# A gated three-branch decoder layer on one core: its output projection in two units of seven products

## The chip, the core and the metric

The kernel runs on one core of a Trainium2 chip. The metric is the device time of one execution in microseconds (us); less is better.

## What is computed

One layer on 512 rows of width 2048, in float32. RMSNorm of the input, one wide input projection (w_in), three mixers of width 1024 whose results are projected to 2048 (w_br_a, w_br_b, w_br_c), a gated sum of the three, the output projection w_o with the residual, and a last RMSNorm. Cut to what matters here:

```python
h = rmsnorm(x, norm_g)
proj = h @ w_in                       # split into ten parts
y_a, y_b, y_c = ...                   # three mixers, each ending in @ w_br_*
g = sigmoid(gates.reshape(bsz, seq, 3, D_MODEL))
merged = g[:, :, 0] * y_a + g[:, :, 1] * y_b + g[:, :, 2] * y_c
x = x + merged @ w_o
return rmsnorm(x, final_g)
```

## The kernel before

Each float32 operand is split into a high and a low part in the type float32r (ScalarE casts the high part, VectorE subtracts to get the low one), and a product is made as three: high by high, low by high, high by low. A matmul has 128 rows of the left operand (the stationary side) and 512 columns of weights; P is 128, CH is 512, a weight block (`rawA`, `rawB`) is 128 by 1024 and holds two steps of 128 channels.

**The input projection** is done in 15 units of 1024 columns. A unit multiplies a 2 by 2 block matrix by a 2 by 2 block matrix in seven products instead of eight (Strassen's way in Winograd's form); `PRODUCTS` (line 58) lists them: 11, s1, s2, s4, s3, 12, 22, with the buffer of each (A or B) and how its weights come: "load" is a plain transfer on SyncE's queue (line 130), "add" a transfer on GpSimd's queue that adds a block to the one in the buffer (line 132), "sum" an addition on VectorE (line 140). `unit` (line 423) runs a product of 8 channel steps by 2 row tiles by 3 matmuls = 48 matmuls, collects results in pairs of PSUM banks (X, Z, V), copies some out (`snap`, ScalarE, line 442), adds others to them (`join`, VectorE, line 447) and hands each finished quarter to a callback (on11, on12, on21, on22). The operands of the left side (the rows of h and their sums and differences) are made once, by `make` and `operand` (lines 349 to 390), and live in `sets`, 28 buffers of the pool `xp`.

**The weights** go through the class `Weights`. `plan` sets when a block is transferred: four blocks ahead of its split, an "add" after the split of what stood in the buffer. `split_to` (line 147) splits a block into `wh` (ScalarE, line 160) and `wl` (VectorE, line 161), two blocks ahead of TensorE and at a raised priority, into three pairs of buffers (`parts`); `place` says into which pool.

**The branches.** `branch` (line 877) multiplies a mixer's result by its projection, 4 groups of 512 columns, 4 row tiles in 4 banks, 96 matmuls a group, and folds in the gates on VectorE (lines 900, 901) into `merged`. The last branch calls `merge_done`, which turns the merged rows into columns on TensorE (`turned`, line 538, 16 transposes a group) and splits them into the high and low operands `m`.

**The output projection** takes the four groups of 512 columns of w_o one after the other: 16 channel steps by 4 row tiles by 3 matmuls, lines 960 to 962. For the last group all weights are split ahead into free buffers, and the row tiles are done one by one (lines 986 to 988), the last one in two halves of 256 columns that have a bank each. `finish` (line 930) adds the residual (line 936), squares and sums on ScalarE (line 937), multiplies by final_g (line 938) and adds up (line 940); after the last group of a row tile comes its root (ScalarE), reciprocal and a Newton step (VectorE), the scaling of its four pieces, two on each engine, and their stores.

**The order on each engine** is set by Tile's scheduler when the program is built, by priority (the order of the code; splits are raised by 300 places) and by its own estimate of when an instruction can start. On the chip each engine then runs its list in that order, and a waiting instruction holds all behind it. `feed` puts queued work (`soon`, `add`) between the steps of the products, at a rate.

## Time and profile before

| | us |
|---|---|
| median of three executions | 1673.27 |
| lowest, highest | 1665.56, 1676.21 |
| the profiled execution, its time | 1667.63 |
| its span (first to last instruction on the core) | 1665.8 |

The rows further down are of the profiled execution, times in us from the start of its span. PE is TensorE (PEld its weight loads), DVE VectorE, ACT ScalarE, POOL GpSimd, SP SyncE; L160 is line 160. Lengths of matmuls overlap, so their pace is read from starts. A name in brackets after an instruction is what ended the idle time of its engine before it.

### The profile page before, as it was taken

The page shows a single profiled execution, that of the slowest core. Times are in us where ns is not written, and L with a number is a line of the kernel's source. Part 1 is how long each engine was busy: PE and PEld are TensorE (multiplying, and loading weights), DVE is VectorE, ACT ScalarE, POOL GpSimd, SP SyncE. Part 2 cuts the span into 40 slices and gives each one's busy share as a digit, 9 for nine tenths or more (in the row PEclk, how much of TensorE's full clock was granted, in tenths as well). Part 3 has the DMA queues.
Part 4 walks back from the last instruction along what each step waited for, and adds up shares of the span by engine and source line. Part 5 has one row for each costly group of instructions (what it writes and reads, how often), then busy time and mean ns, then how long its engine had stood idle before and what let it go on. Part 6 is the DMA issues. An engine that isn't in the chain of part 4 may idle for free.

```text
span 1665.8 us, 19674 instructions
## 1 busy us (share of the span) xinstructions
PE 1633.9 (98%) x7332; PEld 1347.9 (81%) x7332; DVE 1131.3 (68%) x1387; ACT 740.9 (44%) x931; POOL 160.4 (10%) x191
## 2 busy tenths in 40 slices
PE   7899999999999999999999999999999999999997
PEld 5688887888888888888888888888888888888886
DVE  4866699899889969967878885656733544543342
ACT  6756443444444555556645554445622221222322
POOL 1201011110202020101010101111000000000000
PEclk9999999999999999999999999999999999999999
DMA  9978685868777797789989998699984644443302
GB/s 305 237 195 192 176 189 118 227 149 204 153 200 146 200 209 186 175 239 244 296 201 260 227 285 181 176 224 252 240 292 152 197 144 139 127 139 94 105 17 101
DMA packets 111440, 316.04 MB, mean 190 GB/s; under 512 B 12273, under 2 KB 16497, under 8 KB 111345
## 3 DMA queue, kind: packets, MB, share of 16 engines
q1 hardware_dynamic: 63392, 179.50, 33.7%
q0 software_dynamic: 26496, 96.48, 31.3%
q10 hardware_dynamic: 21456, 38.82, 6.4%
q8 instruction: 57, 0.93, 0.2%
q14 instruction: 39, 0.31, 0.1%
HBM read 279.09 MB, written 35.65 MB: 189 GB/s over the span
## 4 chain that ended last, share of the span: by engine, by line
PE 87%; issue 6%; DMA 3%; DVE 2%; POOL 1%; ACT 1%; SPq 0%; ACTq 0%; POOLq 0%; DVEq 0%
PE X L436 12%; PE X L434 12%; PE X L435 11%; PE y L888 5%; PE y L887 5%; PE y L886 5%; PE Z L436 5%; PE Z L434 5%; PE Z L435 5%; PE V L435 3%; PE V L434 3%; PE V L436 3%; PE o L961 3%; PE o L960 3%; PE o L962 3%
## 5 line engine op out<-in xcount | busy, mean ns | idle before, releaser
L161 DVE TENSOR_TENSOR wl<-rawA,wh 128x1024 fp32r<-128x1024 f32 (+1 forms) x281 | 341.6, 1217 | 220.0 <-ACT wh L160 218.2
L160 ACT CAST wh<-rawA 128x1024 fp32r<-128x1024 f32 (+1 forms) x281 | 294.8, 1050 | 408.7 <-PE X L435 113.4
L161 DVE TENSOR_TENSOR wl<-rawB,wh 128x1024 fp32r<-128x1024 f32 x220 | 268.3, 1221 | 237.9 <-ACT wh L160 231.9
L160 ACT CAST wh<-rawB 128x1024 fp32r<-128x1024 f32 x220 | 231.0, 1052 | 358.9 <-PE y L887 102.4
L434 PE MATMUL X<-wh,x 128*128 128x512 f32 x480 | 188.1, 393 | 6.9 <-ACT x L351 6.7
L132 POOL DMA_DIRECT2D rawA<-wts x124 | 107.3, 865 | 896.4 <-DVE wl L161 860.6
L434 PE MATMUL X<-wh,xs 128*128 128x512 f32 x480 | 187.8, 391 | 4.7 <-ACT wh L160 4.6
L435 PE MATMUL X<-wh,x 128*128 128x512 f32 x480 | 187.7, 391 | 1.2 <-DVE x L352 1.2
L435 PE MATMUL Z<-wh,xs 128*128 128x512 f32 x480 | 187.1, 390 | 0.7 <-DVE xs L352 0.7
L434 PE MATMUL Z<-wh,xs 128*128 128x512 f32 x480 | 186.6, 390 | 1.1 <-ACT xs L351 1.1
L435 PE MATMUL X<-wh,xs 128*128 128x512 f32 x480 | 187.3, 390 | 0.0
L436 PE MATMUL X<-wl,xs 128*128 128x512 f32 x480 | 168.8, 391 | 5.8 <-DVE wl L161 5.8
L436 PE MATMUL X<-wl,x 128*128 128x512 f32 x480 | 172.6, 394 | 0.0
L436 PE MATMUL Z<-wl,xs 128*128 128x512 f32 x480 | 169.9, 391 | 0.0
L572 DVE SCALAR_TENSOR_TENSOR conv<-v,prm,conv 128x511 f32<-128x511 f32 (+14 forms) x240 | 168.5, 727 | 0.0
L886 PE MATMUL y<-wh,u 128*128 128x512 f32 x384 | 149.9, 390 | 0.0
L887 PE MATMUL y<-wh,u 128*128 128x512 f32 x384 | 149.7, 390 | 0.0
L888 PE MATMUL y<-wl,u 128*128 128x512 f32 x384 | 149.6, 390 | 0.0
L434 PEld LDWEIGHTS X<-wh,x 128*128 128x128 f32 x480 | 90.2, 189 | 27.3 <-ACT x L351 7.8
L436 PEld LDWEIGHTS X<-wl,xs 128*128 128x128 f32 x480 | 89.6, 188 | 26.7 <-DVE wl L161 8.3
L434 PEld LDWEIGHTS X<-wh,xs 128*128 128x128 f32 x480 | 90.3, 188 | 25.1 <-ACT wh L160 6.3
L435 PEld LDWEIGHTS X<-wh,x 128*128 128x128 f32 x480 | 90.5, 189 | 20.9 <-DVE x L352 2.3
(172 smaller groups left out, 2349.5 us busy)
## 6 DMA issues: line engine op xcount, KB each, us to landing
rawB<-wts SPq DMA_DIRECT2D x160, 512.0 KB, 4.4
rawA<-wts POOLq DMA_DIRECT2D x124, 512.0 KB, 6.7
rawA<-wts SPq DMA_DIRECT2D x99, 512.0 KB, 4.2
rawB<-wts POOLq DMA_DIRECT2D x60, 512.0 KB, 8.8
g<-g SPq DMA_DIRECT2D x48, 256.0 KB, 4.5
d<-turn ACTq DMA_DIRECT2D x32, 256.0 KB, 5.8
g<-snap ACTq DMA_DIRECT2D x24, 256.0 KB, 5.2
g<-gate ACTq DMA_DIRECT2D x24, 256.0 KB, 5.6
```

Of the source, the lines that this page charges most:

```text
L132: self.nc.gpsimd.dma_start(out=self.raw[key], in_=self.src[b], accum_op=ALU.add)
L160: self.nc.scalar.copy(out=h[:, at], in_=raw[:, at])
L161: self.nc.vector.tensor_tensor(out=l[:, at], in0=raw[:, at], in1=h[:, at].bitcast(F32), op=ALU.subtract)
L434: T.matmul(p, lhsT=xh, rhs=h, start=start and k == 0, stop=False, skip_group_check=True)
L435: T.matmul(p, lhsT=xl, rhs=h, start=False, stop=False, skip_group_check=True)
L436: T.matmul(p, lhsT=xh, rhs=l, start=False, stop=k == KB - 1, skip_group_check=True)
L572: V.scalar_tensor_tensor(out=c[:, s:], in0=v[:, : S - s], scalar=pcol(P_BW, i * CONV_B + CONV_B - 1 - s), in1=c[:, s:], op0=ALU.mult, op1= ...
L886: T.matmul(banks[t], lhsT=uh[:, tk], rhs=h, start=k == 0, stop=False)
L887: T.matmul(banks[t], lhsT=ul[:, tk], rhs=h, start=False, stop=False)
L888: T.matmul(banks[t], lhsT=uh[:, tk], rhs=l, start=False, stop=k == KB - 1)
L960: T.matmul(pt[t], lhsT=mh[:, tk], rhs=h, start=k == 0, stop=False)
L961: T.matmul(pt[t], lhsT=ml[:, tk], rhs=h, start=False, stop=False)
```

## The change

The output projection becomes two more units of `PRODUCTS`, each of 1024 columns of w_o, over the merged rows as the left operand, which has 2 by 2 blocks as well: 256 rows by 1024 channels. The rows of w_o are packed in another order (`WO_ROWS`), so that a block's channels come from the column groups 0 and 2, or 1 and 3, and operands can be made as soon as two groups of the last branch are merged. `quarter` turns merged rows into raw quarters (`got`, 256 columns a half, in the pool of small tiles), and `derive` makes an operand from them, as `make` did for the input. In the last branch those of the first two channel pairs are made, in the first output unit those of the others. `finish` takes a sign and adds a product by it. The second unit hands its last product to `last`: its weights are split into buffers of `xp`, tile 2 is finished in one piece, tile 3 in two halves of the same bank.

```diff
 def stages():
     out = []
+    def seven(u, products):
+        for name, tag, what, row, col in products:
+            key = (u, tag, name == "12")
+            out.extend((tag, key + (s,), what, block(u, row, col, s)) for s in range(STEPS))
...
+    for u in range(2):
+        seven(WO_UNIT + u, PRODUCTS)
     return out
...
-    def unit(on11, on12, on21, on22, each=lambda n: None, first=False):
+    def unit(on11, on12, on21, on22, each=lambda n: None, first=False, end=None):
...
+        if end:
+            end(X)
+            return
         run("22", X, False)
...
+    def quarter(cg, i):
+        j, rows = 2 * (cg // 2) + i, cg % 2
+        got = [tmp("m").rearrange("p (c t) -> p c t", c=2) for _ in range(2)]
+        for c in range(2):
+            p = turned([merged[t][cg] for t in range(NT)], 2 * i + c)
+            for h in range(2):
+                A.copy(out=got[h][:, c], in_=p[:, half[h]])
+        quarters[j][rows], quarters[j][rows + 2] = got
     def merge_done(cg):
...
+        if cg == 3:
+            return
+        for i in range(2):
+            soon(0.1, quarter, cg, i)
+        if cg == 1:
+            for j in range(2):
+                for p in FIRST:
+                    add(0.7 if p[0] in ("11", "12", "22") else 1.4, lambda name=p[0], j=j: derive(name, j, *quarters[j]))
...
-    def finish(t, cg, p, lo=0, hi=CH):
+    def finish(t, cg, p, sign, lo=0, hi=CH):
...
-        V.tensor_tensor(out=y[:, at], in0=p, in1=y[:, at], op=ALU.add)
+        V.scalar_tensor_tensor(out=y[:, at], in0=p, scalar=sign, in1=y[:, at], op0=ALU.mult, op1=ALU.add)
...
+    def residual(t, u):
...
+        for cg in (2 * u, 2 * u + 1):
+            nc.sync.dma_start(out=ys[t, cg], in_=xn[t, :, cg * CH : (cg + 1) * CH])
+    def out_each(u):
+        work = {}
+        if u == 0:
+            work[1], work[2] = (lambda: quarter(3, 0)), (lambda: quarter(3, 1))
...
+                work[3 + n] = lambda name=name, j=j: derive(name, j, *quarters[j])
+            work[18] = final_g
...
+    def last(X):
+        ws = [w.next() for _ in range(KB)]
+        for i, p in enumerate(X):
+            step = CH if i == 0 else CH // 2
+            for lo in range(0, CH, step):
+                at = slice(lo, lo + step)
+                for k, (h, l) in enumerate(ws):
...
+                    T.matmul(p[:, at], lhsT=xh, rhs=h[:, at], start=False, stop=False, skip_group_check=True)
...
+                finish(i + 2, 2, p[:, at], 1.0, lo, lo + step)
+            store(i + 2)
+    def place(n, base=len(w.stages) - STEPS):
+        return (xp, "x", "x") if n >= base else (parts, "wh", "wl")
+    w.place = place
+    for u in range(2):
+        def on_left(t, src, u=u):
+            finish(t, 2 * u, src, 1.0)
+            if u and t < 2:
+                store(t)
+        unit(
+            on_left, lambda t, src, u=u: finish(t, 2 * u + 1, src, -1.0), on_left,
+            lambda t, src, u=u: finish(t, 2 * u + 1, src, -1.0), each=out_each(u), end=last if u else None,
+        )
```

Three places in the order of the built programs. First, ScalarE where weights are split ahead of need into buffers of `xp`: before, in the third column group of the output projection (wh494 to wh498 are of the last group).

```order
L160 CAST wh486_11990<-rawA486_11832 128x1024 [waits DMAHW3_49,PE_49,Activation_49]
L937 ACTIVATE sq_862_11972,s_863_11973<-y_856_11854 128x512 [waits DVE_49]
L937 ACTIVATE sq_864_11978,s_865_11979<-y_857_11856 128x512 [waits DVE_49]
L160 CAST wh494_12262<-rawA494_12108 128x1024 [waits DMAHW3_49]
L160 CAST wh487_12020<-rawB487_11870 128x1024 [waits DMAHW0_49,PE_49,Activation_49]
L160 CAST wh495_12268<-rawB495_12146 128x1024 [waits DMAHW0_49]
L160 CAST wh496_12272<-rawA496_12176 128x1024 [waits DMAHW4_49]
L160 CAST wh488_12050<-rawA488_11900 128x1024 [waits DMAHW5_49,PE_49,Activation_49]
L160 CAST wh497_12276<-rawB497_12206 128x1024 [waits DMAHW2_49]
```

The same after, in the second output unit, from the end of s1 to the start of s4's fourth step (wh504 to wh507 are s2's weights, wh508 to wh511 s4's, wh520 to wh523 those of the last product, whose buffers rawA496 to rawA499 get an accumulating transfer first; DMASW is GpSimd's queue).

```order
L170 CAST wh506_12266<-rawA498_12030 128x1024 [waits DVE_49,PE_49]
L450 COPY snap_911_12262<-Z_909_12193 128x512 [waits PE_49]
L170 CAST wh520_12552<-rawA496_11980 128x1024 [waits DMASW0_49]
L170 CAST wh507_12282<-rawA499_12048 128x1024 [waits DVE_49,PE_49]
L170 CAST wh521_12568<-rawA497_11998 128x1024 [waits DMASW1_49]
L170 CAST wh508_12304<-rawB508_12114 128x1024 [waits DVE_49,PE_49]
L170 CAST wh522_12628<-rawA498_12030 128x1024 [waits DMASW2_49]
L170 CAST wh509_12327<-rawB509_12133 128x1024 [waits DVE_49,PE_49]
L170 CAST wh523_12632<-rawA499_12048 128x1024 [waits DMASW3_49,PE_49]
L450 COPY snap_916_12343<-X_904_12111 128x512 [waits PE_49]
L170 CAST wh510_12348<-rawB510_12152 128x1024 [waits DMAHW5_49,DVE_49,PE_49]
L450 COPY snap_917_12344<-X_905_12112 128x512 [waits PE_49]
```

The splits made ahead waited for plain loads (DMAHW); now they wait for accumulating transfers, between casts of s2 and s4.

Second, TensorE at the seam of the two halves of the last row tile: before (o_901 and o_904 are two banks),

```order
L986 MATMUL o_901_12506<-wh499_12284,m_837_11459 128x256
L987 MATMUL o_901_12506<-wh499_12284,m_837_11459 128x256
L988 MATMUL o_901_12506<-wl499_12285,m_837_11459 128x256
L986 MATMUL o_904_12561<-wh492_12178,m_781_10901 128x256 [waits DVE_49]
L987 MATMUL o_904_12561<-wh492_12178,m_781_10901 128x256
L988 MATMUL o_904_12561<-wl492_12179,m_781_10901 128x256
```

and after (X_905 is one bank).

```order
L1027 MATMUL X_905_12112<-wh523_12632,x22_869_11653 128x256
L1028 MATMUL X_905_12112<-wh523_12632,x22_869_11653 128x256
L1029 MATMUL X_905_12112<-wl523_12633,x22_869_11653 128x256
L1027 MATMUL X_905_12112<-wh520_12552,x22_815_11203 128x256 [waits DVE_49]
L1028 MATMUL X_905_12112<-wh520_12552,x22_815_11203 128x256
L1029 MATMUL X_905_12112<-wl520_12553,x22_815_11203 128x256
```

The second half went into a bank of its own; now it follows the first one in the same bank, and waits for VectorE.

Third, VectorE near the end: before, the last row tile, whose halves are read at the first and fourth row,

```order
L936 TENSOR_TENSOR y_885_12294<-o_901_12506,y_885_12294 128x256 [waits PE_49]
L938 TENSOR_TENSOR y_885_12294<-y_885_12294,fgb_825_11391 128x256 [waits Activation_49]
L940 SCALAR_TENSOR_TENSOR ssum3_11706<-s_903_12556,ssum3_11706 128x1
L936 TENSOR_TENSOR y_885_12294<-o_904_12561,y_885_12294 128x256 [waits PE_49]
L938 TENSOR_TENSOR y_885_12294<-y_885_12294,fgb_825_11391 128x256 [waits Activation_49]
L940 SCALAR_TENSOR_TENSOR ssum3_11706<-s_906_12611,ssum3_11706 128x1
L992 RECIPROCAL s_907_12616<-s_908_12617 128x1 [waits Activation_49]
L993 SCALAR_TENSOR_TENSOR s_908_12617<-s_907_12616,ssum3_11706 128x1 [waits DVE_49]
L994 TENSOR_SCALAR s_908_12617<-s_908_12617 128x1 [waits DVE_49]
L995 TENSOR_TENSOR s_907_12616<-s_907_12616,s_908_12617 128x1 [waits DVE_49]
L1001 TENSOR_SCALAR y_841_11576<-y_841_11576,s_907_12616 128x512 [waits DVE_49]
L1001 TENSOR_SCALAR y_873_12132<-y_873_12132,s_907_12616 128x512
```

and after, from the sums of product 12 in the second unit (y_912 is row tile 0, y_913 tile 1, y_915 tile 3; X_905 is the bank of tile 3).

```order
L455 TENSOR_TENSOR snap_906_12188<-V_926_12516,snap_906_12188 128x512 [waits PE_49]
L455 TENSOR_TENSOR snap_907_12189<-V_927_12517,snap_907_12189 128x512 [waits PE_49]
L970 SCALAR_TENSOR_TENSOR y_912_12292<-snap_906_12188,y_912_12292 128x512 [waits DVE_49]
L970 SCALAR_TENSOR_TENSOR y_913_12301<-snap_907_12189,y_913_12301 128x512 [waits DMAHW7_49,DVE_49]
L972 TENSOR_TENSOR y_912_12292<-y_912_12292,fgb_874_11696 128x512 [waits Activation_49]
L974 SCALAR_TENSOR_TENSOR ssum0_11848<-s_929_12586,ssum0_11848 128x1
L970 SCALAR_TENSOR_TENSOR y_915_12323<-X_905_12112,y_915_12323 128x256 [waits DMAHW3_49,PE_49]
L982 RECIPROCAL s_930_12591<-s_931_12592 128x1 [waits Activation_49]
L983 SCALAR_TENSOR_TENSOR s_931_12592<-s_930_12591,ssum0_11848 128x1 [waits DVE_49]
L984 TENSOR_SCALAR s_931_12592<-s_931_12592 128x1 [waits DVE_49]
L972 TENSOR_TENSOR y_913_12301<-y_913_12301,fgb_874_11696 128x512 [waits Activation_49]
L974 SCALAR_TENSOR_TENSOR ssum1_11856<-s_933_12608,ssum1_11856 128x1
```

Before, the closing steps of a row tile stood together; now those of tiles 0 and 1 stand around the read of tile 3's first half.

## Rows read from the trace of the kernel before

**Rows 1.** The page: the span, and engines' busy time, share, instructions.
```profile
span 1665.8 us, 19674 instructions
...
PE 1633.9 (98%) x7332; PEld 1347.9 (81%) x7332; DVE 1131.3 (68%) x1387; ACT 740.9 (44%) x931; POOL 160.4 (10%) x191
```

**Rows 2.** Stretches: start:end, length, busy by engine (instructions), TensorE's granted clock, DMA share, GB/s.
```profile
1000.00:1200.00 200.00, 200.00 (x884) 165.62 (x883) 122.36 (x116) 106.07 (x126) 27.68 (x32) 1.00 0.86 215
1337.00:1480.30 143.30, 143.30 (x657) 118.83 (x656) 69.06 (x88) 32.49 (x37) 0.00 (x0) 1.00 0.48 147
1480.30:1656.90 176.60, 176.60 (x833) 148.17 (x832) 67.59 (x106) 49.32 (x76) 0.00 (x0) 1.00 0.25 78
```

**Rows 3.** Groups by line, 1480.3 to 1666: count, busy us, mean ns, idle before.
```profile
L960 PE MATMUL o<-wh,m 128*128 128x512 f32 x192 | 74.9, 390 | 0.0
...
L986 PE MATMUL o<-wh,m 128*128 128x512 f32 x48 | 18.7, 389 | 0.0
...
L986 PE MATMUL o<-wh,m 128*128 128x256 f32 x32 | 9.1, 283 | 0.0
```

**Rows 4.** TensorE in order of time: start, length, line, tiles.
```profile
1480.34 0.39 PE L960 MATMUL o<-wh,m 128*128 128x512 f32 x1
...
1645.38 0.28 PE L986 MATMUL o<-wh,m 128*128 128x256 f32 x1
...
1656.77 0.28 PE L988 MATMUL o<-wl,m 128*128 128x256 f32 x1
```

**Rows 5.** VectorE in order of time, from 1480.
```profile
1480.38 0.69 DVE L900 TENSOR_TENSOR g<-y,g 128x512 f32<-128x512 f32 x1
1480.99 0.68 DVE L901 TENSOR_TENSOR m<-m,g 128x512 f32<-128x512 f32 x1
...
1482.79 1.22 DVE L161 TENSOR_TENSOR wl<-rawA,wh 128x1024 fp32r<-128x1024 f32 x1
1483.92 0.68 DVE L901 TENSOR_TENSOR m<-m,g 128x512 f32<-128x512 f32 x1
```

**Rows 6.** Line 132, all accumulating transfers of GpSimd's queue: issue to landing, us.
```profile
DMA to landing us min/median/max: 5.3/7.6/12.8
```

**Rows 7.** Last gate unit, in order of time: TensorE's s2 begins, GpSimd's transfers.
```profile
1159.02 0.86 POOL L132 DMA_DIRECT2D rawA<-wts  x1 [14.87 <-DVE wl L161]
...
1159.30 0.39 PE L434 MATMUL X<-wh,xs 128*128 128x512 f32 x1
...
1164.60 0.86 POOL L132 DMA_DIRECT2D rawA<-wts  x1 [1.83 <-DVE wl L161]
```

**Rows 8.** ScalarE in the same stretch.
```profile
1161.99 1.05 ACT L160 CAST wh<-rawA 128x1024 fp32r<-128x1024 f32 x1 [0.63 <-PE X L435]
...
1170.70 1.05 ACT L160 CAST wh<-rawB 128x1024 fp32r<-128x1024 f32 x1
```

**Rows 9.** Landing of the transfers issued at 1159.02 and at 1164.60.
```profile
DMA to landing us min/median/max: 5.6/5.6/5.6
...
DMA to landing us min/median/max: 8.1/8.1/8.1
```

**Rows 10.** VectorE after TensorE's last full products and after its last.
```profile
1645.58 0.69 DVE L936 TENSOR_TENSOR y<-o,y 128x512 f32<-128x512 f32 x1 [6.65 <-PE o L988]
1647.06 0.69 DVE L938 TENSOR_TENSOR y<-y,fgb 128x512 f32<-128x512 f32 x1 [0.79 <-ACT sq L937]
...
1657.09 0.42 DVE L936 TENSOR_TENSOR y<-o,y 128x256 f32<-128x256 f32 x1 [4.26 <-PE o L988]
...
1659.49 0.16 DVE L995 TENSOR_TENSOR s<-s,s 128x1 f32<-128x1 f32 x1
```

**Rows 11.** ScalarE, 1480.3 to 1666: the load of a function table.
```profile
L991 ACT ACT_TABLE_LOAD x1 | 1.3, 1283 | 0.0
```

**Rows 12.** ScalarE at the end, in order of time.
```profile
1659.68 1.33 ACT L999 ACTIVATE y<-y,s 128x512 f32<-128x512 f32 x2 [0.87 <-DVE s L995]
1660.44 0.95 ACTq L1002 DMA_DIRECT2D out<-y  x2
```

More of the change, by code (lines that the diff above doesn't have):

```diff
@@ L364, in less, with derive @@
             V.scalar_tensor_tensor(out=out, in0=in0, scalar=sign, in1=in1, op0=ALU.mult, op1=ALU.subtract)
+    def derive(name, j, x11, x12, x21, x22):
+        if name == "s1":
+            qs[j] = tmp("q").rearrange("p (c t) -> p c t", c=2)
+            less(qs[j], x22, x21)
+        elif name == "s2":
+            less(qs[j], x11, qs[j], -1.0)
+        elif name == "s4":
+            less(qs[j], qs[j], x12, -1.0)
+        elif name == "s3":
+            less(x11, x11, x21)
+        operand(name, j, {"11": x11, "12": x12, "22": x22, "s3": x11}.get(name, qs[j]))
     def make(name, j):
@@ L874, in trunk @@
     merged = [[None] * 4 for _ in range(NT)]
-    m = [None] * KD
     def branch(b, u, done=None):
@@ L943, in finish, with store @@
             V.tensor_scalar(out=ssum[t], in0=s, scalar1=1.0 / D, scalar2=RMS_EPS, op0=ALU.mult, op1=ALU.add)
[L945 to L989 removed]
+    def store(t):
         a, r, n = ssum[t], small(), small()
@@ L1002, in trunk @@
             (nc.scalar if c % 2 else nc.sync).dma_start(out=out[t, :, c * CH : (c + 1) * CH], in_=y)
+    def residual(t, u):
+        if u == 0:
+            ys[t, 0], ys[t, 1] = tmp("y"), tmp("y")
+        else:
+            pair = slot(F32, "y")
+            ys[t, 2], ys[t, 3] = pair[:, 0], pair[:, 1]
+        for cg in (2 * u, 2 * u + 1):
+            nc.sync.dma_start(out=ys[t, cg], in_=xn[t, :, cg * CH : (cg + 1) * CH])
+    def out_each(u):
+        work = {}
+        if u == 0:
+            work[1], work[2] = (lambda: quarter(3, 0)), (lambda: quarter(3, 1))
+            rest = [(p[0], j) for p in FIRST[1:] for j in (2, 3)]
+            rest.sort(key=lambda r: [p[0] for p in PRODUCTS].index(r[0]) if r[0] not in ("12", "22") else 9)
+            for n, (name, j) in enumerate(rest):
+                work[3 + n] = lambda name=name, j=j: derive(name, j, *quarters[j])
+            work[18] = final_g
+        for t in range(NT):
+            work[19 + t] = lambda t=t: residual(t, u)
+        return lambda n: work.get(n, lambda: None)()
@@ new lines, in last @@
+    def last(X):
[5 more added lines that the diff above has]
+                for k, (h, l) in enumerate(ws):
+                    x = sets["22"][k // 2][:, k % 2]
+                    xh, xl = (x[:, o + i * P : o + (i + 1) * P] for o in (0, HT))
+                    end = k == KB - 1
+                    T.matmul(p[:, at], lhsT=xh, rhs=h[:, at], start=False, stop=False, skip_group_check=True)
+                    T.matmul(p[:, at], lhsT=xl, rhs=h[:, at], start=False, stop=False, skip_group_check=True)
+                    T.matmul(p[:, at], lhsT=xh, rhs=l[:, at], start=False, stop=end, skip_group_check=True)
+                finish(i + 2, 2, p[:, at], 1.0, lo, lo + step)
+            store(i + 2)
@@ L1012, in pack, with seven @@
     import numpy as np
-    col = chunked(w_in)
     out = []
-    for _, left, right in UNITS:
-        for row in range(2):
-            for at in (left, right):
-                out.append(col[row * STEPS : (row + 1) * STEPS, at // CH])
+    def seven(col, columns):
+        for left, right in columns:
+            for row in range(2):
+                for at in (left, right):
+                    out.append(col[row * STEPS : (row + 1) * STEPS, at // CH])
+    seven(chunked(w_in), [u[1:] for u in UNITS])
+    for a in (w_a, w_c, w_b):
+        out.append(chunked(a).transpose(1, 0, 2, 3).reshape(-1, P, RAW))
+    rows = w_o.reshape(KD, P, D)[[k for half in WO_ROWS for k in half]].reshape(D, D)
+    seven(chunked(rows), [(RAW * u, RAW * u + CH) for u in range(2)])
     gw = group_w.reshape(len(WINDOWS), 2, P, CG).transpose(0, 2, 1, 3).reshape(2, 2, P, CH)
     out.append(gw.transpose(0, 2, 1, 3).reshape(2, P, RAW))
-    for a in (w_a, w_c, w_b, w_o):
-        out.append(chunked(a).transpose(1, 0, 2, 3).reshape(-1, P, RAW))
     return np.concatenate(out)
```

94 lines of the change are left out of this document (20 added, 74 removed).

## The prediction

> **What bounds the kernel now.** I read the page's busy times first, then the stretches, then groups by line, then single engines in order of time. TensorE is busy 1633.9 of 1665.8 us [rows 1], and the stretches show it without a gap: 200.00 of 200.00 us in a stretch of input units, 143.30 of 143.30 in the last branches, 176.60 of 176.60 in the output projection, each at a granted clock of 1.00, which is the 2.4 GHz level [rows 2]. So whatever stage I look at, its matmuls set the time, and work taken from TensorE is worth its full price as long as nothing new makes it wait. VectorE has much room in the output projection (67.59 us of 176.6) and less in the units (122.36 of 200) [rows 2]. The change makes output units of the first kind out of the second, so I look for waits that the new order can make.
>
> **What goes.** The old projection runs 3 x 192 + 3 x 48 = 720 products of 512 columns and 3 x 32 = 96 of 256 [rows 3]. The busy lengths (390 and 283 ns) overlap; the pace is read from starts. From 1645.38 to 1656.77 the 96 short ones take 11.39/95 = 0.120 us each [rows 4]. From 1480.34 to 1645.38 there are 165.04 us for 720 long ones and 16 transposes [rows 4]; twelve long ones in a row stand 2.72 us after one another, 0.2266 each, 163.15 in all, which leaves 0.118 for a transpose. The new projection has 2 x 7 x 8 x 6 = 672 products, 24 of them cut in two halves: 648 long and 48 short. The transposes stay 64 in all, 16 of them after the branch. Removed: 72 x 0.2266 + 48 x 0.120 = 16.3 + 5.8 = **22.1 us** of TensorE, all of it on the path. The program is the same, engine by engine, until the second column group of the last branch, so nothing before some 1413 us moves.
>
> **What I cost at nothing.** Sixteen operands and eight differences are made in the last branch. VectorE is busy there 69.06 of 143.30 us and ScalarE 32.49 [rows 2]; 24 more operations of 0.605 on VectorE, 14.5 us, fit into the last two column groups (43 us) beside their 16 merges and 8 splits (19 us). If they did not, the weights' low halves would come late by the overhang. The transfers: the output stage goes from 32 plain loads of 512 KB to 24 plain and 24 adding, where the engines of the DMA are busy a quarter of the time (share 0.25 [rows 2]). The residual's rows move from ScalarE's queue to SyncE's, ahead of weights of later products there; the first unit's wait for its last operands, some 34 us after the branch, and what stands behind them is needed 20 us later still.
>
> **What comes: the vector work of the first output unit.** Call the end of the branch on TensorE 0. VectorE is through with the last merges and one weight half at 1483.92 + 0.68 - 1480.34 = 4.26 [rows 4, 5]; the same eight merges stand there after the change. From there to the low half of s4's first weights the new order has 14 operations of 1024 columns (10 splits, 4 sums) and 20 of 512 (operands and differences). Their starts follow at 1.13 and 0.605 us [rows 5]: 15.8 + 12.1 = 27.9, and 2.5 more while the first s1 weights wait for a free buffer, so 34.7. TensorE asks for that half after 3 x 48 products, 16 transposes and four products more: 32.6 + 1.9 + 0.8 = 35.3. Just in time. By the full lengths (1.22 and 0.68) it would be 17.1 + 13.6 = 30.7, plus 2.5: 37.5, late by 2.2. Bounds 0 and 2.2; starts are what a queue runs by, so I take **0.5**. ScalarE's casts are shorter and hide behind this. The second unit has no operands to make.
>
> **What comes: casts that wait for transfers.** In the second output unit the casts of the last product's weights (wh520 to wh523) stand on ScalarE between those of s2 and s4, and each waits for an accumulating transfer that starts only when s2's own split of the same buffer is done. ScalarE is in order: behind them stand s2's fourth cast, then those of s4 and the snapshots, and TensorE needs these. Before the change such transfers have three products of time. Let s2 begin on TensorE at 0 and a transfer land L after issue. In the last gate unit the first is issued at 1159.02 - 1159.30 = -0.28 and the fourth at 5.3 [rows 7]; s2's fourth cast starts at 2.69 there, s4's third at 11.40 [rows 8]. Now the first held cast ends at L + 0.8, s2's fourth at L + 1.75, its low half on VectorE at L + 3.1; TensorE needs that after three steps of 2.72 and four products more, 8.16 + 0.9 = 9.06, so it waits A = L - 5.95 (none if negative). That low half releases the fourth transfer at L + 3.4, landing at 2L + 3.4; then wh523, a snapshot and s4's third cast take 2.6, to 2L + 6.0, needed after s2's four steps and two of s4, at 10.88 + 5.44 + A: wait B = 2L - 10.3 - A. Together 2L - 10.3. Over all transfers of that line L is 5.3 at least, 7.6 in the middle, 12.8 at most [rows 6]: 0.3, 4.9 and 15.3 us. In the last gate unit the first landed after 5.6 and the fourth after 8.1 [rows 9], by which A is 0 and B 3.4; all at 5.6 give 0.9. There the gates' spills ran too (DMA share 0.86 [rows 2]); the output units have none. I take **2.5**, bounds 0.3 and 15.3.
>
> The Trainium skill, DMA: Bandwidth & Descriptors, section Anatomy of one DMA (SWDGE, the GpSimd path), gives an estimate of 2.0 us plus the bytes over 436 GB/s, 3.2 us for 512 KB; the hold would then be nothing and the sum 2.5 us better. The rows, with 5.3 as the least, say otherwise for transfers that add, and decide.
>
> **What comes: the last product without cover.** Elsewhere product 12 stands between s3 and 22, so the sums that read s3's banks are hidden. In the second unit the new order runs 22 right behind s3. Its first matmul waits until a 512-column sum has read the bank: some 0.7 us of sum [rows 5], of which bank one's lead of three matmuls hides most; one split of 1.22 stands before it. Bounds 0 and 1.2; I take **0.5**.
>
> **What comes: the tail.** The old tail is 1665.8 - 1656.77 = 9.03 us after the last matmul's start [rows 1, 4]. It closed one row tile at a time, 48 products (10.9 us) apart. Now the order on TensorE is 22 for tile 2, product 12 for tiles 0 and 1, then the two halves for tile 3; so tiles 0 to 3 all close in the last 20 us, in an order fixed on VectorE and ScalarE. Let product 12 end at 0. VectorE sums two banks and adds into tiles 0 and 1 (four operations, the third from 0.8); 1.48 after the third's start it may multiply tile 0 (the square lies between, 1645.58 to 1647.06 [rows 10]): 2.3 to 3.05 with its small sum. Only then comes the read of tile 3's first half, to 3.5, and the second half's matmuls, in the same bank, wait for it: they start at 3.55, while the 21 short products before end at 2.5. Last matmul at 6.3, for 5.3 unhindered. ScalarE meanwhile loads a table (1.28 [rows 11]) to 3.6, takes tile 0's root and tile 1's square; VectorE has tile 0's factor at 5.5. ScalarE scales tile 0 (1.33 for two [rows 12]) to 6.9 and only then squares tile 2, to 7.66; VectorE multiplies tile 2 to 8.35, scales tile 1 to 9.15, sums to 9.3; ScalarE's two stores of tile 1 (0.95 [rows 12]) hold tile 2's root to 9.7; tile 3's squares end at 10.9, its sum at 11.4, its root at 11.65; VectorE scales tile 2 (0.88) before it takes tile 3's reciprocal at 12.5, factor at 13.3; ScalarE's stores of tile 2 go out to 13.45, then it scales tile 3. From that to the end it took 1665.8 - 1659.68 = 6.12 [rows 1, 12]: 19.6. Unhindered: 5.3 + 9.03 = 14.3. Loss **5.3**. Lower bound 1.0 (the wait for the bank alone, both queues keeping pace), upper 7.5 (sixteen stores of 256 KB in 12 us instead of four in the last 6, two us more for the last).
>
> On the bank, the Trainium skill, PSUM — Partial Sum Buffer, section PSUM bank collisions raise a hardware error, says that accesses of two engines are to be kept apart by bank and quadrant, not by address. By address alone the second half need not wait and the last matmul would come 1.0 earlier; no row of before shows this wait, since its two halves had banks of their own.
>
> **Sum.** -22.1 + 0.5 + 2.5 + 0.5 + 5.3 = **-13.3 us**. Against the profiled execution, 1667.63 (span 1665.8 and 1.83 around it), that gives 1654.3. That execution lies below the median of the three others (1673.27; 1665.56 to 1676.21); the mean of all four is 1670.7, and 1670.7 - 13.3 = **1657.4**, my figure. What a measurement of this kernel can tell from no change is about 1%, 16.7 us.
>
> **Rivals.**
> 1. All is hidden: the tail loses only the bank's 1.0, the transfers land in 5.3 (0.3). 22.1 - 1.3 = 20.8 off: 1649.9. For it: VectorE's share in the stage, 67.59 of 176.6 [rows 2], and room on ScalarE. Against it: the order of the tail on two in-order queues, which no room elsewhere undoes.
> 2. Slower than before: the held casts of the second unit. Each us of L costs two, so with the other losses at 6.3 the gain is gone at 2L - 10.3 = 15.8, L = 13.05. At L = 16 the loss is 21.7 + 6.3 - 22.1 = +5.9: 1676.6; over 1% needs L = 21.4. For it: 12.8 occurs [rows 6], and the four transfers feed on one another. Against it: few other transfers run there.
> 3. VectorE becomes the bound in the first unit: full lengths and a late first cast, 2.2, and again in the s4 of that unit, 2.2, with a tail of 7.5 and L at 7.6: -22.1 + 4.4 + 4.9 + 0.5 + 7.5 = -4.8, 1665.9.
>
> **How the numbers follow.** Forecast 0.50, rival 1 0.25, rival 3 0.17, rival 2 0.08. Low end: losses of 0, 0.3, 0 and 3.5 on the lowest execution, 1665.56 - 18.3 = 1647. High end: rival 3's -4.8 on the median, 1673.27 - 4.8, rounded up to 1669; it leaves out rival 2 and the edges. Faster by over 1%: all of rival 1 and 0.08 of the forecast, 0.33. Slower by over 1%: most of rival 2, 0.06 with rounding. Within 1%: 0.61.
>
> **What would show it.** TensorE's line of the summing products gains 624 matmuls and the old output lines' 816 go; it has no gap up to the second unit's s2. There ScalarE idles before casts of line 170, released by rawA transfers, and TensorE waits some 2.5 us around s2's fourth and s4's third weights; if neither engine waits, that term falls. At the end TensorE waits about 1 us on line 970 before its last 24 short matmuls, and the last of them starts 13 us before the end of the span, not 9. If that distance stays 9, the tail term is wrong; if VectorE's line 171 delays TensorE in the first unit by over 2 us, the vector term is.

## The result and the profile after

The changed kernel takes 1655.99 us (median of six; 1653.03 to 1658.91), the kernel before 1670.12 on the same occasions (1665.23 to 1676.21): a ratio of 0.9924, 95% interval 0.9908 to 0.9941. That is 0.8% faster, below the 1% that the prediction called the limit of what can be told, though the interval is clear of 1. The predicted figure was 1657.4 in a range of 1647 to 1669.

The page of the changed kernel, in the places of [rows 1]:

```profile
span 1654.1 us, 19662 instructions
...
PE 1617.2 (98%) x7212; PEld 1332.0 (81%) x7212; DVE 1191.8 (72%) x1459; ACT 786.3 (48%) x1011; POOL 181.6 (11%) x215
```

The stretches that answer to [rows 2]: the last branch, and the output projection from its first matmul to its last.

```profile
1337.00:1481.10 144.10, 144.10 (x662) 119.53 (x660) 76.50 (x100) 41.70 (x66) 1.73 (x2) 1.00 0.39 115
1481.10:1640.50 159.40, 157.17 (x713) 128.26 (x711) 117.12 (x152) 81.64 (x119) 19.07 (x22) 1.00 0.65 154
```

TensorE is no longer without a gap there (157.17 of 159.40), VectorE's work has gone from 67.59 to 117.12 us and the share of the DMA engines from 0.25 to 0.65. Both have lost much of their room, and the question is which of them TensorE met. Its own rows tell, in order of time: the stage's first matmul, the three largest waits with the matmul before each, its last.

```profile
1481.10 0.39 PE L442 MATMUL X<-wh,x 128*128 128x512 f32 x1
...
1526.25 0.39 PE L444 MATMUL Z<-wl,xs 128*128 128x512 f32 x1
1527.66 0.50 PE L442 MATMUL X<-wh,xs 128*128 128x512 f32 x1 [1.02 <-ACT wh L170]
...
1599.60 0.39 PE L444 MATMUL Z<-wl,xs 128*128 128x512 f32 x1
1600.14 0.50 PE L442 MATMUL Z<-wh,xs 128*128 128x512 f32 x1 [0.16 <-ACT wh L170]
...
1636.51 0.28 PE L1029 MATMUL X<-wl,x 128*128 128x256 f32 x1
1637.55 0.39 PE L1027 MATMUL X<-wh,x 128*128 128x256 f32 x1 [0.76 <-DVE y L970]
...
1640.40 0.28 PE L1029 MATMUL X<-wl,x 128*128 128x256 f32 x1
```

From first to last it is 159.30 us, before 176.43 [rows 4]: 17.1 of the 22.1 us removed are won there. A matmul should start 0.23 after the one before it (0.12 behind a half), so the three waits are 1.2 us at 1527.66, at the first weight of s3 in the first unit; 0.3 at 1600.14, in s4 of the second unit; and 0.9 at 1637.55, the seam of row tile 3. In both products the weights then stay just in time for a while. Measured by the lengths of products (48 matmuls should take 10.88), the first place costs 1.18 before s3 and 1.45 within it, the second 0.81 in all. From the last matmul's start to the end of the span there are now 1654.1 - 1640.40 = 13.70 us; it was 9.03. The whole stage, from its first matmul to the end of the span, went from 185.46 to 173.00: 12.5 us less, where the sum said 13.3. The stage began 0.76 later than before, and in the runs below it begins between 1478.87 and 1483.96; what lies ahead of it differs by 5 us between profiled executions, so from here on I compare stages.

What held the first place: GpSimd's transfers for s3 (first and last), and their times from issue to landing.

```profile
1515.89 0.86 POOL L142 DMA_DIRECT2D rawB<-wts  x1 [4.34 <-DVE wl L171]
...
1520.90 0.89 POOL L142 DMA_DIRECT2D rawB<-wts  x1 [1.82 <-DVE wl L171]
```

```profile
DMA to landing us min/median/max: 10.6/10.6/10.6
...
DMA to landing us min/median/max: 14.7/14.7/14.7
```

The first is issued at 1515.89, 0.3 us after s4 began on TensorE, and lands 10.6 us later, when s4 is through. The windows say why it took so long; the last two columns are the busy share of the DMA engines and GB/s (a packet's whole time is counted in the window where it starts, so a share can pass 1).

```profile
1500.00:1505.00 5.00, 5.00 (x24) 4.14 (x23) 5.00 (x7) 1.42 (x2) 0.81 (x1) 1.00 0.28 100
...
1510.00:1530.00 20.00, 18.92 (x83) 15.02 (x82) 10.37 (x13) 8.61 (x13) 4.35 (x5) 1.00 1.05 245
1530.00:1535.00 5.00, 4.94 (x22) 3.37 (x20) 4.21 (x6) 2.53 (x4) 0.00 (x0) 1.00 1.05 269
```

From 1510 on the engines of the DMA are full. Under way are the last product's accumulating transfers (issued 1504 to 1511; their weights are used on TensorE from 1550.87 on), s3's four behind them, final_g and the residual's rows.

What held the second place: ScalarE in the second unit, the four casts that wait for transfers (rawA, the last product's) and the cast of s4's third weights (rawB) behind the last of them.

```profile
1586.90 2.00 ACT L170 CAST wh<-rawA 128x1024 fp32r<-128x1024 f32 x2 [1.86 <-DMA rawA<-wts]
...
1592.07 1.05 ACT L170 CAST wh<-rawA 128x1024 fp32r<-128x1024 f32 x1 [0.50 <-DMA rawA<-wts]
...
1597.61 1.05 ACT L170 CAST wh<-rawA 128x1024 fp32r<-128x1024 f32 x1 [3.54 <-DMA rawA<-wts]
...
1599.05 1.05 ACT L170 CAST wh<-rawB 128x1024 fp32r<-128x1024 f32 x1
```

The four transfers took this long to land:

```profile
DMA to landing us min/median/max: 5.6/6.1/6.9
```

The cast at 1597.61 had ScalarE idle for 3.54 us; s4's third stands behind it and a snapshot, at 1599.05, and TensorE takes its weights at 1600.14. This is the hold of the prediction, with its price smaller.

And the end, ScalarE: the table load, tile 3's first square, its last scalings and stores.

```profile
1636.38 1.28 ACT L981 ACT_TABLE_LOAD   x1
...
1643.17 0.37 ACT L971 ACTIVATE sq<-y 128x256 f32<-128x256 f32 x1
...
1646.53 1.33 ACT L989 ACTIVATE y<-y,s 128x512 f32<-128x512 f32 x2 [0.42 <-DVE s L985]
1647.41 1.61 ACTq L992 DMA_DIRECT2D out<-y  x2
```

Between 1636.4 and 1644.8 ScalarE takes roots, squares and scalings of tiles 0, 1 and 2 ahead of tile 3's and between them.

### The profile page after: what moved, and what is told of

The parts are those of the page before. It is cut to its first block, busy times and chain, and to the rows that moved or that the text cites. A ratio compares the mean times of both kernels' runs of the same rounds, so it can differ in the third digit from the quotient of the medians.

```text
span 1654.1 us, 19662 instructions
## 1 busy us (share of the span) xinstructions
PE 1617.2 (98%) x7212; PEld 1332.0 (81%) x7212; DVE 1191.8 (72%) x1459; ACT 786.3 (48%) x1011; POOL 181.6 (11%) x215
## 4 chain that ended last, share of the span: by engine, by line
PE 76%; issue 12%; DMA 5%; DVE 2%; POOL 2%; ACT 2%; SPq 0%; POOLq 0%; ACTq 0%; DVEq 0%
PE X L444 12%; PE X L442 12%; PE X L443 12%; PE Z L444 5%; PE Z L442 5%; PE Z L443 5%; PE y L897 4%; PE y L896 4%; PE y L898 4%; PE V L443 3%; PE V L442 3%; PE V L444 3%; DMA rawB<-wts 2%; DMA rawA<-wts 2%; POOL rawA L142 2%
## 5 line engine op out<-in xcount | busy, mean ns | idle before, releaser
L171 DVE TENSOR_TENSOR wl<-rawA,wh 128x1024 fp32r<-128x1024 f32 (+1 forms) x297 | 361.3, 1218 | 195.6 <-ACT wh L170 191.0
L170 ACT CAST wh<-rawA 128x1024 fp32r<-128x1024 f32 (+1 forms) x297 | 311.8, 1051 | 397.8 <-PE X L443 118.2
L171 DVE TENSOR_TENSOR wl<-rawB,wh 128x1024 fp32r<-128x1024 f32 x228 | 277.9, 1222 | 206.7 <-ACT wh L170 204.3
L170 ACT CAST wh<-rawB 128x1024 fp32r<-128x1024 f32 x228 | 238.9, 1052 | 332.5 <-PE y L897 97.6
L142 POOL DMA_DIRECT2D rawA<-wts x140 | 121.4, 867 | 1285.1 <-DVE wl L171 1249.2
L442 PE MATMUL X<-wh,x 128*128 128x512 f32 x528 | 208.2, 396 | 8.3 <-ACT x L361 8.1
L442 PE MATMUL X<-wh,xs 128*128 128x512 f32 x544 | 213.1, 392 | 3.2 <-ACT wh L170 3.1
L442 PE MATMUL Z<-wh,xs 128*128 128x512 f32 x544 | 212.2, 391 | 1.5 <-ACT xs L361 1.4
L443 PE MATMUL Z<-wh,xs 128*128 128x512 f32 x544 | 212.7, 391 | 0.7 <-DVE xs L362 0.7
L443 PE MATMUL X<-wh,xs 128*128 128x512 f32 x544 | 212.6, 391 | 0.0
L443 PE MATMUL X<-wh,x 128*128 128x512 f32 x528 | 207.3, 393 | 0.1
L444 PE MATMUL X<-wl,xs 128*128 128x512 f32 x544 | 191.9, 392 | 5.1 <-DVE wl L171 5.0
L444 PE MATMUL Z<-wl,xs 128*128 128x512 f32 x544 | 192.5, 391 | 2.6 <-DVE wl L171 2.5
L444 PE MATMUL X<-wl,x 128*128 128x512 f32 x528 | 191.6, 396 | 0.0
L442 PEld LDWEIGHTS X<-wh,x 128*128 128x128 f32 x528 | 100.1, 190 | 30.3 <-ACT x L361 8.8
L444 PEld LDWEIGHTS Z<-wl,xs 128*128 128x128 f32 x544 | 102.1, 188 | 24.7 <-DVE wl L171 3.4
```

What stands on the lines that cost most here:

```text
L142: self.nc.gpsimd.dma_start(out=self.raw[key], in_=self.src[b], accum_op=ALU.add)
L170: self.nc.scalar.copy(out=h[:, at], in_=raw[:, at])
L171: self.nc.vector.tensor_tensor(out=l[:, at], in0=raw[:, at], in1=h[:, at].bitcast(F32), op=ALU.subtract)
L442: T.matmul(p, lhsT=xh, rhs=h, start=start and k == 0, stop=False, skip_group_check=True)
L443: T.matmul(p, lhsT=xl, rhs=h, start=False, stop=False, skip_group_check=True)
L444: T.matmul(p, lhsT=xh, rhs=l, start=False, stop=k == KB - 1, skip_group_check=True)
```

## The experiments

Two losses could be told apart by what stands on which queue; two edits do that (e1, e2), two treat the tail (e3, e4), three put together what helped.

**e1: the last product's transfers start late.**

```diff
 def plan(self):
-    out.append((max(n - self.load_ahead, before[key] + 1), n))
+    at = max(n - self.load_ahead, before[key] + 1)
+    u, s = divmod(n - (len(self.stages) - 14 * STEPS), 7 * STEPS)
+    if u >= 0 and s >= 6 * STEPS:
+        at = n - s + 16
+        self.late.add(n)
+    out.append((at, n))
...
 def transfer(self):
+    if n in self.late:
+        a = self.raw[key][:, :1]
+        self.nc.vector.scalar_tensor_tensor(out=a, in0=self.mark[:, :1].bitcast(F32), scalar=0.0, in1=a, op0=ALU.mult, op1=ALU.add)
```

(`mark` is the low half that was split last; the operation adds zero times its first column. The edit is cut to what matters. Eleven lines more move L142 to L153 and L170 to L181, twelve move the lines further down.)

> Edit: in both output units the four accumulating transfers of the last product (22) may start only after the last split of s4 (a tiny VectorE operation on one column of the buffer carries the wait); all else as in the changed kernel. Theory A, transfers crowd: in the first output unit these four (512 KB each, needed 22 us later than s3's) stand on GpSimd's queue ahead of s3's four, which then land 10.6 to 14.7 us after issue, and TensorE loses 2.6 us in s3 (1.18 before its first weight, 1.45 in the rest). With them behind, s3's land in 9 us or less and the 2.6 us become 0.8 or less. In the second unit the held casts leave the place between s2's and s4's: the 1.1 us lost in s4 and s3 there become 0.3 or less. Span 3 us shorter, about 1651. Theory B, the vector and scalar work of the first unit is too late: s4's splits and so s3's transfers start as late as before (0.3 us after s4 begins, in the gate units 2.9 before), and 2.0 us or more of the 2.6 remain; span 1653. Third case: the four come too late for product 22 in the second unit, directly behind s3, and TensorE waits there 1 to 3 us; span as before, 1654.

Measured: ratio to the kernel before 0.9955 (0.9933 to 0.9977), stage 178.8 us, 5.8 longer than the changed kernel's; the span, 1661.6, is longer than each of the three cases expected, and the intervals of the two ratios just overlap. In the first unit theory A holds. s3's first transfer is issued 0.3 us after s4 begins, exactly as late as in the changed kernel, and the four land like this:

```profile
1517.63 0.86 POOL L153 DMA_DIRECT2D rawB<-wts  x1 [28.24 <-DVE wl L182]
```

```profile
DMA to landing us min/median/max: 5.4/7.4/9.3
```

s4 and s3 then take 10.88 us each; the 2.6 us are gone, with VectorE's and ScalarE's work as it was. From s4's first matmul to product 12's the window reads:

```profile
1517.33:1539.09 21.76, 21.76 (x98) 18.02 (x96) 15.34 (x23) 10.28 (x15) 7.05 (x8) 1.00 0.96 210
```

The DMA engines are nearly as full here (0.96) as over the same products in the changed kernel (1.00), and TensorE does not wait. So it was less the fullness that cost the 2.6 us than the order: the transfers needed first stood behind those needed last. In the second unit the third case came, harder than expected. TensorE in s3 and at the first matmul of 22, then ScalarE at that time:

```profile
1611.15 0.50 PE L454 MATMUL X<-wh,xs 128*128 128x512 f32 x1 [1.18 <-ACT wh L181]
...
1613.20 0.50 PE L456 MATMUL X<-wl,xs 128*128 128x512 f32 x1 [0.86 <-DVE wl L182]
...
1622.21 0.80 PE L1039 MATMUL X<-wh,x 128*128 128x512 f32 x1 [3.69 <-DVE snap L467]
```

```profile
1601.62 1.05 ACT L181 CAST wh<-rawB 128x1024 fp32r<-128x1024 f32 x1 [1.67 <-PE Z L455]
1609.10 1.05 ACT L181 CAST wh<-rawA 128x1024 fp32r<-128x1024 f32 x1 [6.43 <-DMA rawA<-wts]
1610.05 1.04 ACT L181 CAST wh<-rawB 128x1024 fp32r<-128x1024 f32 x1
```

The late transfers moved the casts that wait for them from between s2's and s4's to between s3's. The four, issued within 2 us, landed one by one:

```profile
DMA to landing us min/median/max: 5.2/13.0/17.0
```

(the least, 5.2, is one of s3's; the others took 9.7 to 17.0). ScalarE stood 6.43 us at the first, with s3's third cast behind it at 1610.05. TensorE waited 1.18 for that cast and 0.86 for a low half behind it, and 3.69 at product 22, because VectorE came to read s3's bank only after these splits; from the start of s3 to that of 22 it took 17.84 us for 10.88. So a held cast is a real price on this queue, 7 us in one product. And there is more behind the wait of 3.69 us: the granted clock (third column from the end) is at 0.50, the 1.2 GHz level, and from 1622.81 to 1627.93 twelve matmuls take 5.12 us, 0.427 each instead of 0.227, 2.4 us more.

```profile
1622.00:1628.00 6.00, 5.79 (x14) 4.54 (x15) 4.53 (x9) 1.34 (x4) 0.00 (x0) 0.50 0.00 0
```

**e2: less vector work before s4's splits.**

```diff
 for n, (name, j) in enumerate(rest):
+    if name in ("12", "22"):
+        sets[name][j] = sets[name][j - 2]
+        continue
```

> Edit: in the first output unit the four operands of products 12 and 22 for the last two channel pairs are not made (the operands of the first two pairs stand in their place, so these parts of the output are those of other channels); it takes four casts (2.2 us) and four subtractions (2.5 us) from just before s4's splits, and no transfer. Theory A, transfers crowd: s4's splits come 2 us earlier, but the accumulating transfers of s3 meet the same crowd and land 11 us or more after issue; of the 2.6 us that TensorE loses in s3 1.5 or more remain. Theory B, vector work too late: s3's transfers start 2 to 2.5 us earlier, land in the same time or less, and 0.6 us or less of the 2.6 remain; span 1652.

Measured: ratio 0.9947 (0.9931 to 0.9963), stage 175.6 us. s3's transfers were issued from 1513.52 on, 2.1 us before s4 began, 2.4 earlier than in the changed kernel, and TensorE waited longer:

```profile
DMA to landing us min/median/max: 13.6/15.1/15.9
```

```profile
1530.36 0.50 PE L442 MATMUL X<-wh,xs 128*128 128x512 f32 x1 [3.68 <-ACT wh L170]
```

They landed in 13.6 to 15.9 us where it had been 10.6 to 14.7. The edit has a side that I had not seen: four buffers of `xp` stay free, and the second unit's residual rows come forward, as SyncE's row tells (16 transfers where there were 8, so 2 MB more in the crowd):

```profile
1483.69 46.96 SPq L1001 DMA_DIRECT2D y<-xn  x16
```

The loss is 3.85 us before s3 and 2.11 within it, but the transfers made only part of that. The first landed 13.6 us after 1513.52, at 1527.1. ScalarE cast its block 2 us later, because two squares stood before the cast and waited for VectorE:

```profile
1528.04 0.60 ACT L971 ACTIVATE sq<-y 128x512 f32<-128x512 f32 x1 [8.65 <-DVE y L970]
...
1529.28 1.03 ACT L170 CAST wh<-rawB 128x1024 fp32r<-128x1024 f32 x1
```

And behind TensorE's wait the granted clock is at 0.50 again; eight starts from 1531.62 to 1535.07 take 3.45 us where 1.81 would do, 1.6 of the 2.11:

```profile
1532.00:1535.00 3.00, 3.00 (x8) 2.32 (x7) 1.07 (x2) 1.04 (x1) 0.00 (x0) 0.50 1.04 265
```

That leaves some 2.3 us, no more than the changed kernel loses, so it is not shown that the added 2 MB hurt. Several things changed at once and e2 alone decides little. What it does show is against theory B: issued 2.4 us earlier, the first transfer landed 0.7 us later than in the changed kernel (1526.46). e1 decides.

**e3: tiles 0 and 1 closed early.**

```diff
-        seven(WO_UNIT + u, PRODUCTS)
+        seven(WO_UNIT + u, FIRST if u else PRODUCTS)
...
-            work[19 + t] = lambda t=t: residual(t, u)
+            work[(8 if u else 19) + t] = lambda t=t: residual(t, u)
...
+        def on_right(t, src, u=u):
+            finish(t, 2 * u + 1, src, -1.0)
+            if u and t < 2:
+                store(t)
-        unit(... each=out_each(u), end=last if u else None)
+        unit(on_left, on_right, on_left, on_right, each=out_each(u), first=u == 1, end=last if u else None)
```

(`on_left` no longer calls `store`.)

> Edit: the second output unit runs its products in the order of the very first input unit (11, 12, s1, s2, s4, s3, 22), so that row tiles 0 and 1 are closed after s4 and only tiles 2 and 3 at the end; the residual's rows of that unit are asked for 11 steps earlier, and s2's weights come by accumulating transfers instead of a sum on VectorE. Theory of the tail (four tiles closing in the last 20 us on two queues): the distance from the last matmul's start to the end of the span falls from 13.7 to 9.0 to 10.0 us, the wait of 0.8 us at the seam of tile 3 stays; TensorE's casts of 22 are still held between s2's and s4's, 1 to 2 us lost. Span 3.5 to 4.5 shorter, about 1650. Rival: the distance is set by the stores and the last tile's own chain; it stays above 12.5, and the span within 1.5 us of 1654. Second rival: s2's four new accumulating transfers come late and TensorE waits 2 us or more at s2; span 1652 or more.

Measured: ratio 0.9885 (0.9867 to 0.9903); span 1647.8. TensorE at the seam and at its last matmul, and ScalarE with tile 0's first store and tile 3's last scalings and stores:

```profile
1636.01 0.39 PE L1027 MATMUL X<-wh,x 128*128 128x256 f32 x1 [0.52 <-DVE y L970]
...
1638.87 0.28 PE L1029 MATMUL X<-wl,x 128*128 128x256 f32 x1
```

```profile
1624.57 0.96 ACTq L992 DMA_DIRECT2D out<-y  x2
...
1641.78 1.33 ACT L989 ACTIVATE y<-y,s 128x512 f32<-128x512 f32 x2 [0.87 <-DVE s L985]
1642.53 0.95 ACTq L992 DMA_DIRECT2D out<-y  x2
```

Tile 0's stores go out at 1624.57, 14 us before the last matmul. From the last matmul to the end there are 8.93 us instead of 13.70: the whole loss behind the last matmul is gone, and with it is shown that it came from four tiles that close at once (the edit's other two changes lie earlier: in the changed kernel the residual's rows had landed by 1579.61 already). The first unit still loses 1.42 + 1.35. In the second every product up to s4 takes 10.88, so the held casts, which I expected to cost 1 to 2 us, cost nothing in this order.

**e4: tile 3 in one piece.**

```diff
-            step = CH if i == 0 else CH // 2
+            step = CH
```

> Edit: row tile 3 of the last product is done in one piece of 512 columns instead of two halves in one bank. The 48 short matmuls (0.120 each, 5.8 us) become 24 long ones (5.4), and the seam, where TensorE waits 0.8 to 0.9 us for VectorE's read of the first half, is gone: the last matmul starts 1.2 us earlier, 39.2 from the end of s3 to 38 or so. Theory 1, the distance to the end is set by the queues (ScalarE and VectorE still closing tiles 1 and 2): the last tile's larger pieces hide there, the distance grows by 1.2 at most and the span is the same within 0.5. Theory 2, it is set by tile 3's own chain: larger pieces cost 0.3 + 0.2 + 0.3, the span is 0.4 shorter. Against both: if the seam cost nothing, the last matmul comes only 0.3 earlier.

Measured: ratio 0.9932 (0.9906 to 0.9957; two executions), span 1653.6. The last matmul, and ScalarE's scalings of tiles 2 and 3:

```profile
1637.66 0.39 PE L1029 MATMUL X<-wl,x 128*128 128x512 f32 x1
```

```profile
1643.15 1.32 ACT L989 ACTIVATE y<-y,s 128x512 f32<-128x512 f32 x2
...
1645.56 1.33 ACT L989 ACTIVATE y<-y,s 128x512 f32<-128x512 f32 x2 [0.87 <-DVE s L985]
```

The stage's TensorE time falls from 159.30 to 157.03 and the distance to the end rises from 13.70 to 15.94: stage 172.97, as in the changed kernel. That is theory 1, though the distance grew by more than the 1.2 us it allowed: the queues set the end, and TensorE may be earlier by 2.3 us for nothing. Of these 2.3, 0.8 were not the edit's: s4 of the second unit took 10.88 here, though the casts are held as in the changed kernel, with landings of 5.4 to 6.3 us where the last one took 6.9.

**e5, e6, e7: both, and two forms of the last tile.** e5 is e3 with e1's late start for the first unit alone (`u == 0` for `u >= 0`). e6 and e7 change `last`:

```diff
-        for i, p in enumerate(X):
-            step = CH if i == 0 else CH // 2
-            for lo in range(0, CH, step):
+        for i, lo, hi in (1, 0, CH // 2), (0, 0, CH), (1, CH // 2, CH):
...
```

in e6; in e7 the step is CH, as in e4.

> Edit: the order of products of e3 in the second output unit, and the late start of the last product's transfers of e1, in the first unit alone. If the two losses are separate, they add: the second unit and the tail as in e3 (158.4 us from the first to the last matmul of the output stage, 8.9 from there to the end), less the 1.4 + 1.3 us that TensorE lost around and in s3 of the first unit: 155.6, span 1645, time about 1647, some 2.7 below e3 and 1.3% below the kernel before the change. If the late transfers only shift the crowd to the first unit's product 22 (needed 22 us after s3), TensorE waits there 1 us or more and the span stays at 1647.

> Edit: e5, and the last product done as first half of tile 3, tile 2, second half of tile 3; built, the order on TensorE is 21 matmuls of tile 2, the first half, the last 3 of tile 2, the second half. The read of the first half has 3 matmuls (0.68 us) to hide behind: the wait of 0.5 to 0.8 us at the seam becomes 0.2 or less, the last matmul starts 0.5 to 0.6 earlier. Tile 2 now closes 2.9 us before the last matmul and not 5.8: if the queues have room, the distance to the end stays at 8.9 and the span is 0.5 shorter than e5's; if tile 2's closing steps stand in the way of tile 3's, the distance grows by 0.5 to 1.5 and nothing is won.

> Edit: e5, and tile 3 in one piece of 512 columns. The seam's wait (0.5 to 0.8) and 0.3 of short matmuls go from TensorE. The distance to the end, now tile 3's own chain, grows by the longer pieces: 0.27 for the sum, 0.2 for the square, 0.27 for the product, 0.8 in all with waits: 9.7. Span within 0.3 of e5's. In e4, where queues set the end, the same edit moved the last matmul 2 us earlier and the span by 0.5; if the distance grows here by 1.5 or more as well, queues set it here too.

Measured, in ratio to the kernel before: e5 0.9888 (0.9874 to 0.9903), e6 0.9907 (0.9890 to 0.9924), e7 0.9888 (0.9872 to 0.9905). e5's TensorE at the seam and at its last matmul, and the stretch of the crowd, where TensorE is now busy for all 30.00 us at a DMA share (last but one column) of 0.89:

```profile
1632.13 0.39 PE L1039 MATMUL X<-wh,x 128*128 128x256 f32 x1 [0.52 <-DVE y L982]
...
1634.98 0.28 PE L1041 MATMUL X<-wl,x 128*128 128x256 f32 x1
```

```profile
1505.00:1535.00 30.00, 30.00 (x135) 24.82 (x134) 23.48 (x34) 18.23 (x27) 7.04 (x8) 1.00 0.89 215
```

The stages, each from TensorE's first and last row and the page's span, of one profiled execution for each kernel:

| | first matmul | last matmul | span | first to last | last to end | stage |
|---|---|---|---|---|---|---|
| before | 1480.34 | 1656.77 | 1665.8 | 176.43 | 9.03 | 185.46 |
| after | 1481.10 | 1640.40 | 1654.1 | 159.30 | 13.70 | 173.00 |
| e1 | 1482.83 | 1648.33 | 1661.6 | 165.50 | 13.27 | 178.77 |
| e2 | 1481.13 | 1642.92 | 1656.7 | 161.79 | 13.78 | 175.57 |
| e3 | 1480.51 | 1638.87 | 1647.8 | 158.36 | 8.93 | 167.29 |
| e4 | 1480.63 | 1637.66 | 1653.6 | 157.03 | 15.94 | 172.97 |
| e5 | 1479.41 | 1634.98 | 1643.9 | 155.57 | 8.92 | 164.49 |
| e6 | 1483.96 | 1638.84 | 1649.2 | 154.88 | 10.36 | 165.24 |
| e7 | 1478.87 | 1633.23 | 1643.0 | 154.36 | 9.77 | 164.13 |

e5's 155.57 is the 155.6 expected: the losses are separate and add up, and the first unit's product 22 does not wait. e6 takes the seam's wait away (no start in the stage is late by 0.4 any more; 0.7 won) and gives twice that back (1.44), because tile 2's closing steps stand before tile 3's: ScalarE scales tile 2 at 1640.13, between tile 3's last square (1639.62) and its root (1641.37), 0.7 us, and from tile 3's scalings to the end it takes 0.8 longer than in e5. e7 has no halves; its last matmul comes 1.2 earlier and its end 0.85 later behind it: 0.4 less, where 0.3 at most was expected. With one profile each that is not shown as a gain: s4 alone differed by 0.8 between the changed kernel and e4, where nothing had been changed. The times of e3, e5 and e7 can't be told apart (their intervals overlap), only the rows do that; all three are clear of the changed kernel's interval. By their rows e5 and e7 are the versions to keep: 1.1% below the kernel before.

## Why the prediction was right, point by point

The figure (1657.4) and the sign were right, and the 13.3 us of the sum stand beside 12.5 in the stage. Behind that the terms came out like this.

**What goes, 22.1.** Right. e7 has whole tiles only: 672 x 0.2266 + 16 x 0.118 = 154.2, measured 154.36, of which 0.27 is the wait at product 22. No other time is hidden in TensorE's count.

**The vector work of the first unit, 0.5.** The term was nothing. VectorE in the changed kernel reaches s4's low halves here (three in a row, 1.13 apart):

```profile
1514.38 3.54 DVE L171 TENSOR_TENSOR wl<-rawB,wh 128x1024 fp32r<-128x1024 f32 x3
```

The first is ready at 1514.38 + 1.22 - 1481.10 = 34.5, where the working had 34.7, and with the same vector work e1 loses nothing in that unit. But 2.63 us were lost there, and the step that failed is another: "The transfers: the output stage goes from 32 plain loads of 512 KB to 24 plain and 24 adding, where the engines of the DMA are busy a quarter of the time", costed at nothing. I took the share of before as room, and did not ask when, and in which order, the new transfers start. The 24 adding ones come in groups behind splits, and in the first unit two groups, final_g and the residual meet within 20 us: share 1.05, landings of 10.6 to 14.7 us. e1 and e5 show the cost of the order by putting four of them behind s3's: landings of 5.2 to 9.3 us and no wait. That VectorE's late splits had a part in it is not excluded: s3's transfers start 3 us later against TensorE than in the gate units, which costs nothing in e1's order, and no run has the changed kernel's order without it. My sentence that the residual's move to SyncE's queue costs nothing belongs to the same step, but what the residual adds was not measured by itself.

**Held casts, 2.5 of 0.3 to 15.3.** The mechanism was right (the rows of ScalarE above; 6.43 us of standing in e1), the term too big: 0.8 us in the changed kernel, none in e4, where the fourth transfer took 0.6 us less. Two sizes were off. The landings were 5.6 to 6.9, not the median of 7.6 over the whole program; and the first transfer was issued at 1581.23, 2.3 us before s2's begin at 1583.51, where I had taken 0.3 from the gate unit, so that everything behind it came 2 us sooner. The Trainium skill's estimate that the prediction weighed (DMA: Bandwidth & Descriptors, Anatomy of one DMA; 3.2 us for 512 KB) stays below every landing of an accumulating transfer in these runs' output stages, the least of which is 5.1.

**The last product without cover, 0.5.** Right in size: the first matmul of 22 starts 0.27 late, and the next 0.1. e1 shows the price when VectorE is behind: a wait of 3.69 us, and 2.4 more at the lower clock.

**The tail, 5.3.** Right. The seam cost 0.9 where I had 1.0, and the distance grew by 4.7; 5.6 in all. The last matmul starts 13.7 us before the end (predicted 13): ScalarE's last scalings begin 6.13 after it, where the working had 13.45 - 6.3 = 7.15, and from there to the end it took 7.57 where it had 6.12, so the queues were quicker and the stores slower than I took them. e3 gives all but the seam back, e4 shows that work on TensorE's side is worth nothing there.

So two terms were too big by 2.2 together (vector work 0.5, held casts 1.7), one of 2.6 was missing, and the tail was 0.3 too small: the sum came out within 0.8 us because errors of both signs met. Of the signs that the prediction named, TensorE's first gap came before s2 of the second unit, which it had excluded; and that gap was on a cast (L170), with shorter ones on VectorE's L171 behind it. Rival 1 failed by the tail, rival 3 because VectorE was not the bound, rival 2 because no landing in the changed kernel's second unit came near 13 us.

What was not tried: whether the second half in the same bank must wait at all. The Trainium skill (PSUM — Partial Sum Buffer, PSUM bank collisions raise a hardware error) says that two engines are to be kept apart by bank. No run here starts a second half in the same bank without the wait.

## What to carry to other kernels

A low mean share of the DMA engines is no room for new transfers: list when each becomes free to start, and look for the stretch where they meet; what is needed last should not stand on the queue ahead of what is needed first. On an in-order engine a cast that waits for a transfer charges its wait to all behind it, so moving the transfer without moving the cast only moves the bill (e1). A long wait of TensorE can cost more than its length: in e1 and e2, behind waits of 3.7 us, it ran at a granted clock of 0.50 for 2.4 and 1.6 us more. And before the end, ask which row tiles close together: an order of the same products that closes half of them earlier was worth more than a third of the whole change (4.8 us behind the last matmul against 12.5).

## What I had not expected of the hardware

The accumulating transfers on GpSimd's queue fill the DMA engines more than the plain ones on SyncE's. The page's third part of the changed kernel (packets, MB, share of 16 engines): q0 carries GpSimd's 208 transfers, all of them accumulating, q1 SyncE's plain ones.

```profile
q0 software_dynamic: 29952, 109.07, 35.9%
q1 hardware_dynamic: 64544, 179.50, 33.6%
```

That is 0.329% per MB against 0.187%, 1.76 times as much. How much of it is the accumulation and how much the queue these runs do not tell, since every transfer of q0 accumulates and none of q1 does. And several issued together land one after another: in e1 the four of one product, issued within 2 us, released ScalarE's casts at 1609.10, 1612.90, 1615.46 and 1617.96, some 3 us apart for 512 KB each.
